# A two-block transformer kernel: comparisons ahead of the weight split, and the mixer's and the layer boundaries' weight work in another order

## The chip, the cores and the metric

One core of one Trainium2 chip runs the whole kernel in one launch. The time is the device time of the launch in microseconds (us), taken as the median over runs; lower is better.

## The reference, cut to what matters

256 tokens of width 1024 in fp32 go through two blocks.

```python
def reference(x, ...):
    h = x
    for i in range(2):                        # first block
        m = diff_attention(h) if i == 0 else short_gated_conv(h)
        h = layer_norm(ALPHA * h + m)
        h = layer_norm(ALPHA * h + swiglu(h))
    x = h                                     # second block
    x = x + parallel_mixer(rms_norm(x))       # 4 mLSTM heads, 8 stick-breaking heads, then w_out
    x = x + memory_cross_attention(rms_norm(x), rms_norm(mem))
    x = x + peer_ffn(rms_norm(x))
    return rms_norm(x)

def peer_ffn(xt):                             # 16384 experts, 8 heads, 16 experts per head and token
    experts, gates = top16(product_keys(xt @ wq))
    act = gelu(einsum('cd,ced->ce', xt, u[experts])) * gates
    return einsum('ce,ced->cd', act, v[experts])
```

`parallel_mixer` puts its mLSTM queries and keys through a causal depthwise convolution of four taps with a bias, then silu; both kinds of head are normalised per head before `w_out`. `mem` is a second sequence of 256 tokens, normalised and projected to keys and values of the cross-attention.

## The kernel before, in words

**Weights.** All weight matrices come as one stream (class `Stream`, L198 to L260) of 1 MB chunks, in a fixed plan. The SyncE queue (SP) loads a chunk into one of two `raw` buffers; each half of it, 128 x 1024, is cast by ScalarE (ACT) into a high part `wh` (L231), and the rest `wl` = raw - wh is formed by VectorE (DVE) or GpSimd (POOL), whichever `W.sub[k]` names for half k (L243). A product is three matmuls, high x high, high x low, low x high (L329, L330, L331). `W.split(n)` brings the split up to half n, `W.pre(n)` the cast alone; asking for half n splits `W.look` halves further on (0, 1 or 2). `wh` and `wl` have three buffers each, and a chunk's buffer is loaded again once both its halves are split.

**Order.** Every engine runs its instructions in the order in which the program writes them; there is no other scheduler. So a line that is written earlier stands ahead on its engine, and an instruction that waits holds up all behind it.

**First block.** The loop over `st` (L776) takes one attention head per step: `qk_proj` projects, `qk_rot` shuffles columns on DVE (L647) and multiplies with the rope tables on POOL (L649, L651, L653), `scores` and `soft` follow one step later. Beside it run `mem_norm` (norm of one half of `mem`), `lam` (the scalar lambda) and `to_T(mem_in)`, which transposes `mem` on TensorE (PE) and splits it into `mT` (high `mTh`, low `mTl`, L378). At the end of each layer, `finish` ends the last matmuls of token half 0, then of half 1, while the norm of half 0 runs, with projections of the memory (`mem_k0`, `mem_k1`, `mem_v`) in between to keep PE at work; `finish_any` (L505) and `finish_two` (L475) set which weights are split there, on which engine.

**Between the blocks.** After the second feed-forward layer, two DMAs on the POOL queue (L965) copy `mT` (2 x 1 MB) to the buffers of an old activation, so that the memory of `mT` can be used for the mixer's tiles.

**Mixer.** `mqk` (L1045) projects one mLSTM head's query and key, and does the convolution on DVE: the first tap and the bias as `tensor_scalar` (L1059), the three others as `scalar_tensor_tensor` (L1062). Meanwhile the halves k = 0 of the weights are split on POOL. `ml_norm` scales the mLSTM heads (L1131), `sb_norm` norms the stick-breaking heads with a product on POOL (L1192) and one on DVE (L1198), `mem_v(2)` projects the memory beside it, and `w_out` ends in a layer boundary again.

**PEER.** All 16384 expert rows of `u` are multiplied with the tokens, in 64 chunks of two halves. The gates of most tokens are scattered by POOL into a zeroed table in DRAM; the gates of the last 128 tokens are made in the last halves of the `u` loop instead, four tokens at a time, in three steps per half: `hot_make` compares an iota with the experts' row and column numbers on DVE (`oi`, L1571; `oj`, L1574), `hot_mm` multiplies the two one-hot tiles on PE (L1581) and writes the result into the table `big`: its finished columns are multiplied on DVE (L1584), the others copied by ACT (L1585). `gelu` (L1592, L1595, L1596) puts the activations into `big`, with a product on DVE or POOL (`late`, run by `gated()`). These halves are called the hot stage below. The loop's order in one half is: split of the weights to come (in `w(k)`), gelu of the last chunk, the product, then `hot_make` for the next half and `hot_mm` of the half before:

```python
            w(k)
...
            proj_stat(ps[:, k * 256:k * 256 + 256], w, k, xT)
...
                if e < 33:
                    hot_make(e - 1)
                gated()
                if e > 1:
                    hot_mm(e - 2, 2 * c)
```

The `v` rows follow as 64 more chunks, with the table `big` as the other factor.

## Time and profile before

| what | value |
|---|---|
| median of 3 runs | 1720.41 us (1719.59 to 1721.41) |
| the profiled execution | 1723.32 us, of it the span 1721.5 us |
| granted TensorE clock, mean over the span | 0.992 of full |
| PE busy with matmuls | 1656.5 us, 96% of the span |
| DVE busy | 1175.8 us, 68% |
| ACT busy | 815.0 us, 47% |
| POOL busy | 483.2 us, 28% |
| DMA | 317.48 MB, 184 GB/s over the span |

The profile is of one execution, 0.17% longer than the median. The shares are averages over stages with different limits: where PE idles is read from stretches of the trace, and what it waits for from the releaser that the trace puts down at each idle time. A matmul row gives the start and the modelled length; matmuls overlap, so the distance between starts tells what one costs.

### The profile page before, as it was taken

How to read it: one execution, taken by the hardware profiler on the slowest of the kernel's cores; microseconds unless marked ns; L12 is line 12 of the kernel's file. 1: busy time of each engine (PE TensorE's matmuls, PEld its weight loads, DVE VectorE, ACT ScalarE, POOL GpSimd, SP SyncE). 2: the span in 40 equal slices, each digit the busy share in tenths (PEclk: the TensorE clock that was granted, in tenths of full speed). 3: DMA queues.
4: the chain of work that ended last, by engine and by line, in shares of the span. 5: the costliest groups of instructions: out<-in, count | busy, mean ns of one | idle time of the engine just before them, and what ended most of it. 6: DMA issues, size and time to landing. Idle time of an engine off the chain costs nothing.

```text
span 1721.5 us, 27583 instructions
## 1 busy us (share of the span) xinstructions
PE 1656.5 (96%) x11013; PEld 1505.5 (87%) x11013; DVE 1175.8 (68%) x2069; ACT 815.0 (47%) x1260; POOL 483.2 (28%) x446
## 2 busy tenths in 40 slices
PE   8899999999999998998999999999888999999997
PEld 7888999899999977887989999999887888888886
DVE  5897554667654564776558889888777666666665
ACT  5564444434444444564445545445332444444544
POOL 0542000200200022203037887788501211111111
PEclk9999999999999999999999999999999999999999
DMA  7346776455555545434355676766433566666664
GB/s 272 137 140 231 256 237 234 172 208 200 207 182 196 177 166 192 164 104 145 122 193 167 178 196 176 193 181 188 100 121 101 188 219 206 209 219 209 207 217 171
DMA packets 80416, 317.48 MB, mean 184 GB/s; under 512 B 25120, under 2 KB 41760, under 8 KB 45344
## 3 DMA queue, kind: packets, MB, share of 16 engines
q1 hardware_dynamic: 59120, 304.38, 51.7%
q0 software_dynamic: 20736, 10.56, 4.1%
q8 instruction: 86, 1.41, 0.3%
q10 hardware_dynamic: 432, 0.79, 0.1%
q14 instruction: 42, 0.34, 0.1%
HBM read 303.04 MB, written 10.55 MB: 182 GB/s over the span
## 4 chain that ended last, share of the span: by engine, by line
PE 47%; DVE 8%; issue 3%; ACT 3%; POOL 1%; DMA 1%; POOLq 0%; DVEq 0%; ACTq 0%
PE acc L331 8%; PE acc L330 7%; PE acc L329 7%; PE mm L329 7%; PE mm L331 7%; PE mm L330 7%; ACT wh L231 2%; DVE oj L1574 2%; DVE oi L1571 1%; DVE big L1584 1%; DVE wl L243 1%; DMA xTl<-mTl 1%; DVE qkm L1062 1%; POOL wl L243 0%; PE mm L1460 0%
## 5 line engine op out<-in xcount | busy, mean ns | idle before, releaser
L243 DVE TENSOR_TENSOR wl<-raw,wh 128x1024 fp32r<-128x1024 f32 (+1 forms) x511 | 631.5, 1254 | 301.6 <-ACT wh L231 300.3
L231 ACT ACTIVATE wh<-raw 128x1024 fp32r<-128x1024 f32 (+1 forms) x537 | 552.6, 1053 | 377.4 <-PE acc L331 181.7
L329 PE MATMUL mm<-xTh,wh 128*128 128x256 f32 x2328 | 660.2, 284 | 1.1 <-DVE mTl L378 1.1
L331 PE MATMUL mm<-xTh,wl 128*128 128x256 f32 x2328 | 655.8, 282 | 1.8 <-DVE wl L243 1.5
L330 PE MATMUL mm<-xTl,wh 128*128 128x256 f32 x2328 | 655.3, 281 | 0.0
L329 PEld LDWEIGHTS mm<-xTh,wh 128*128 128x128 f32 x2328 | 441.6, 190 | 3.9 <-DVE mTl L378 1.5
L331 PEld LDWEIGHTS mm<-xTh,wl 128*128 128x128 f32 x2328 | 441.3, 190 | 2.7 <-DVE wl L243 1.9
L330 PEld LDWEIGHTS mm<-xTl,wh 128*128 128x128 f32 x2328 | 441.5, 190 | 0.9
L1492 POOL DMA_INDIRECT gd<-slots,idx x128 | 259.9, 2030 | 68.9 <-issue 32.3
L329 PE MATMUL acc<-wh,xTh 128*128 128x512 f32 x632 | 249.7, 395 | 0.0
L330 PE MATMUL acc<-wl,xTh 128*128 128x512 f32 x632 | 249.2, 394 | 0.2 <-DVE wl L243 0.2
L243 POOL TENSOR_TENSOR wl<-raw,wh 128x1024 fp32r<-128x1024 f32 x26 | 64.6, 2491 | 566.8 <-ACT wh L231 565.2
L331 PE MATMUL acc<-wh,xTh 128*128 128x512 f32 x504 | 201.1, 399 | 0.0
L330 PEld LDWEIGHTS acc<-wl,xTh 128*128 128x128 f32 x632 | 119.1, 188 | 30.2 <-DVE wl L243 0.8
L329 PEld LDWEIGHTS acc<-wh,xTh 128*128 128x128 f32 x632 | 119.0, 188 | 28.7 <-issue 0.7
L1539 POOL TENSOR_TENSOR big<-big,oj 128x256 f32<-128x256 f32 x64 | 57.5, 898 | 290.3 <-DMA oj<-gd 290.3
L331 PEld LDWEIGHTS acc<-wh,xTh 128*128 128x128 f32 x504 | 94.6, 188 | 21.7
L880 DVE TENSOR_TENSOR sil<-sil,mm 128x256 f32<-128x256 f32 x44 | 18.5, 421 | 102.7 <-ACT sil L879 102.7
L879 ACT ACTIVATE sil<-mm 128x256 f32<-128x256 f32 x44 | 16.9, 385 | 148.4 <-PE mm L331 148.4
L362 DVE TENSOR_TENSOR xTh<-big,xTh 128x256 fp32r<-128x256 f32 x126 | 79.4, 630 | 0.0
L1491 POOL MEMSET spacer<- 1x1 f32 x128 | 78.9, 616 | 0.0
L330 PE MATMUL acc<-wl,hTh 128*128 128x512 f32 x176 | 69.6, 395 | 0.0
(388 smaller groups left out, 1844.2 us busy)
## 6 DMA issues: line engine op xcount, KB each, us to landing
raw<-in_ws_dram SPq DMA_DIRECT2D x131, 1024.0 KB, 5.1
raw<-in_us_dram SPq DMA_DIRECT2D x64, 1024.0 KB, 5.1
raw<-in_vs_dram SPq DMA_DIRECT2D x64, 1024.0 KB, 4.9
gd<-zt SPq DMA_DIRECT2D x32, 256.0 KB, 6.9
raw<-in_pq_dram SPq DMA_DIRECT2D x8, 1024.0 KB, 4.9
oj<-gd SPq DMA_DIRECT2D x64, 128.0 KB, 4.8
gb<-in_vec_dram POOLq DMA_DIRECT2D x12, 512.0 KB, 7.1
gd<-slots,idx POOLq DMA_INDIRECT x128, 4.0
```

The costliest lines, as they stand in the source:

```text
L231: self.nc.scalar.activation(h[:, s], self.R[i][:, k * HW:(k + 1) * HW][:, s], AF.Copy)
L243: self.sub[k].tensor_tensor(l[:, s], self.R[i][:, k * HW:(k + 1) * HW][:, s], h.bitcast(F32)[:, s], op=OP.subtract)
L329: P.matmul(ps, lh, rh, start=first, stop=False)
L330: P.matmul(ps, lh, rl, start=False, stop=False)
L331: P.matmul(ps, ll, rh, start=False, stop=last)
L362: V.tensor_tensor(l, src, h.bitcast(F32), op=OP.subtract)
L880: V.tensor_tensor(s, s, pg[:, 256:], op=OP.mult)
L1062: V.scalar_tensor_tensor(y[:, a, :], pad[:, a, j:j + 256], cols[:, 24 + 4 * ft + j:25 + 4 * ft + j], y[:, a, :], op0=OP.mult, op1=OP.add)
L1491: G.memset(spacer, 0.0)
L1492: d = G.indirect_dma_start(out=gd, out_offset=bass.IndirectOffsetOnAxis(ap=idx[:, h, k:k + 1], axis=0), in_=gate[:, 0, h, k:k + 1], in_off ...
L1539: G.tensor_tensor(b, b, GT.pop(c), op=OP.mult)
L1574: V.tensor_scalar(oj[:, i, :], iota, ET[:, 1, t:t + 1], ET[:, 2, t:t + 1], op0=OP.is_equal, op1=OP.mult)
```

## The change

Nothing is computed otherwise; work is put elsewhere in the order, on another engine, or in other pieces.

1. A half that POOL splits is subtracted in four pieces of 256 columns instead of one instruction of 1024 (`Stream.split`).
2. `finish_two` no longer splits the first half of the next chunk on POOL ahead of the norm of token half 0; it is split later with the second half.
3. `finish_any`, in its `early` form, only casts there, and subtracts after the norm's first part of both token halves.
4. In the first attention heads the column shuffle of head 0 stands ahead of the weight split, of the memory's second norm and of lambda; the transposes of `mem` go ahead of a weight split and the softmax's second part.
5. The copy of `mT` is issued ahead of the last layer boundary of the first block instead of behind it.
6. In `mqk` the first tap is done by ACT, and all weight halves are split on DVE.
7. `ml_norm` is split in two: token half 1 ahead of `sb_z`, half 0 behind it; `sb_c(5)` goes ahead of a transpose.
8. `sb_norm` multiplies in four pieces on POOL; the weights next to it are split on DVE, with `W.look` at 1 for `mem_v(2)`.
9. In the hot stage `hot_make` stands ahead of `w(k)`, and so ahead of the weight split.

```diff
@@ -239,7 +239,10 @@
             h, l = self.T[self.ns]
-            for s in self.parts(self.ns):
+            ps = self.parts(self.ns)
+            if self.sub[k] is self.nc.gpsimd:
+                ps = [slice(q, q + 256) for q in range(0, HW, 256)]
+            for s in ps:
                 self.sub[k].tensor_tensor(l[:, s], self.R[i][:, k * HW:(k + 1) * HW][:, s], h.bitcast(F32)[:, s],
@@ -475,8 +478,6 @@
         last_mm(acc, items, 1, 1)
-        W.sub = [G, G]
-        W.split(2 * W.i + 3)
         W.sub = [G, G]
@@ -519,11 +520,14 @@
             last_mm(acc, items, 1, 1)
-            W.split(2 * W.i + first + early)
+            W.pre(2 * W.i + first + early)
         fa(1, 0)
...
         fa(1, 1)
+        if early:
+            W.sub = [V, G]
+            W.split(W.np - 1)
         if callable(src0):
@@ -772,13 +776,10 @@
     mem_norm(0)
-    mem_norm(1)
     for st in range(8 + 5):
...
             qk_proj(st)
-        if st == 0:
-            lam()
         if st == 8:
@@ -800,6 +801,8 @@
             W.split(2 * W.i + 4)
+            mem_norm(1)
+            lam()
         if 0 <= st - 1 < 8:
@@ -807,13 +810,13 @@
                 pv_n(st - 4)
+            if st in (1, 2):
+                to_T(mem_in[st - 1], st - 1, mT)
             W.split(2 * W.i + 4)
...
             soft(st - 1)
-        if st in (1, 2):
-            to_T(mem_in[st - 1], st - 1, mT)
 
@@ -958,11 +961,12 @@
 
+    mT2 = new_xT()
+    for k in range(2):
+        G.dma_start(mT2[k], mT[k])
     finish(acc, items, lambda t, nb: ln_a(t, nb, acc, h3), ln_rms, xT, [lambda: mem_v(0)], [lambda: mem_v(1)], True, early=0)
     f2ctx.close()
-    mTo, mT = mT, new_xT()
-    for k in range(2):
-        G.dma_start(mT[k], mTo[k])
+    mT = mT2
     mctx.close()
@@ -1056,8 +1060,8 @@
             ft = a * 4 + h
-            V.tensor_scalar(y[:, a, :], pad[:, a, 0:256], cols[:, 24 + 4 * ft:25 + 4 * ft], cols[:, 56 + ft:57 + ft],
-                            op0=OP.mult, op1=OP.add)
+            A.activation(y[:, a, :], pad[:, a, 0:256], AF.Identity, bias=cols[:, 56 + ft:57 + ft],
+                         scale=cols[:, 24 + 4 * ft:25 + 4 * ft])
             for j in range(1, 4):
@@ -1123,12 +1127,10 @@
 
-    def ml_norm(ss):
-        rs = inv_sqrt(ss, 8, "rs8")
-        for t in (1, 0):
-            for h in range(4):
-                hs = slice(h * 128, h * 128 + 128)
-                V.tensor_scalar(mixed[:, t, hs], mixed[:, t, hs], rs[:, 4 * t + h:4 * t + h + 1], None, op0=OP.mult)
+    def ml_norm(rs, t):
+        for h in range(4):
+            hs = slice(h * 128, h * 128 + 128)
+            V.tensor_scalar(mixed[:, t, hs], mixed[:, t, hs], rs[:, 4 * t + h:4 * t + h + 1], None, op0=OP.mult)
 
@@ -1189,7 +1191,8 @@
             A.activation(sq, mixed[:, t, 512:], AF.Square)
-            G.tensor_tensor(mixed[:, t, 512:], mixed[:, t, 512:], gmx[:, 512:], op=OP.mult)
+            for c in (slice(512, 768), slice(768, 1024)):
+                G.tensor_tensor(mixed[:, t, c], mixed[:, t, c], gmx[:, c], op=OP.mult)
             V.tensor_reduce(ss[:, 8 * t:8 * t + 8], sq.rearrange("p (a b) -> p a b", a=8), axis=AX.X, op=OP.add)
@@ -1207,7 +1210,6 @@
         A.activation(vx[:, t, :, 0:128], pss[t].rearrange("p (a b) -> p a b", a=4), AF.Copy)
-    W.sub = [G, V]
     for h in range(4):
@@ -1230,7 +1232,8 @@
         if hs == 6:
-            ml_norm(ss8)
+            rs8 = inv_sqrt(ss8, 8, "rs8")
+            ml_norm(rs8, 1)
         i, k = divmod(hs - 2, 2)
@@ -1238,6 +1241,8 @@
                 sb_z(i)
+                if hs == 6:
+                    ml_norm(rs8, 0)
             elif i < 2:
@@ -1252,8 +1257,8 @@
     sb_c(4)
+    sb_c(5)
     to_T_half(mixed[:, 0, :], 0, mxT, 0)
-    sb_c(5)
     acc = acc_banks()
@@ -1266,12 +1271,12 @@
     sb_v(7)
-    W.sub = [G, V]
     sb_norm()
+    W.look = 1
     mem_v(2)
-    W.sub = [V, V]
     for t in range(2):
         to_T_half(mixed[:, t, :], t, mxT, 1)
+    W.look = 2
     items = o_items(mxT, "wout", 2)
@@ -1607,6 +1612,9 @@
         for k in range(2):
+            e = 2 * c + k - HOT0
+            if 1 <= e < 33:
+                hot_make(e - 1)
             w(k)
@@ -1618,18 +1626,13 @@
             pump(CRED1)
-            e = 2 * c + k - HOT0
             if e >= 0:
...
                 hot_T()
-            if 1 <= e < 34:
-                if e < 33:
-                    hot_make(e - 1)
-                gated()
-                if e > 1:
-                    hot_mm(e - 2, 2 * c)
             gated()
+            if 2 <= e < 34:
+                hot_mm(e - 2, 2 * c)
         pend.append(lambda c=c, ps=ps: gelu(c, ps))
```

On DVE in the hot stage the kernel before has, from the end of one step to the start of the next, the last comparisons of a step (`oj`), the late product of the gelu (`gx`), the product into `big`, the weight split and the next comparison (`oi`):

```order
L1574 TENSOR_SCALAR oj<-cst,ET 128x128 x4
L1596 TENSOR_TENSOR big<-big,gx 128x2x44
L1584 TENSOR_TENSOR big<-big,acc_13539 128x104x4
L243 TENSOR_TENSOR wl<-raw,wh 128x1024
L1571 TENSOR_TENSOR oi<-cst,ET 128x512
```

In the changed kernel, at the same place on DVE:

```order
L1601 TENSOR_TENSOR big<-big,gx 128x2x44
L1589 TENSOR_TENSOR big<-big,acc_13595 128x104x4
L1576 TENSOR_TENSOR oi<-cst,ET 128x512
L1579 TENSOR_SCALAR oj<-cst,ET 128x128 x4
L246 TENSOR_TENSOR wl<-raw,wh 128x1024
```

The comparisons now stand between the product into `big` and the next split, where the split followed the product at once.

On POOL at the end of the first block, the kernel before has the loads of norm vectors (`gb`), a weight split, the norms of the two token halves (`rs`, `h`), and the copy behind them:

```order
L301 DMA gb<-in_vec_dram 128x1024 x3
L243 TENSOR_TENSOR wl<-raw,wh 128x1024
L320 TENSOR_TENSOR rs_6562<-rs1a,nhalf 128x1
L426 TENSOR_TENSOR h<-r,gb 128x512 x2
L320 TENSOR_TENSOR rs_6606<-rs1a,nhalf 128x1
L243 TENSOR_TENSOR wl<-raw,wh 128x1024
L320 TENSOR_TENSOR rs_6624<-ssa,nhalf 128x1
L320 TENSOR_TENSOR rs_6635<-ssa,nhalf 128x1
L243 TENSOR_TENSOR wl<-raw,wh 128x1024 x2
L965 DMA xTh_6705<-mTh 128x2048
L965 DMA xTl_6706<-mTl 128x2048
```

In the changed kernel POOL has:

```order
L304 DMA gb<-in_vec_dram 128x1024 x3
L966 DMA xTh_6514<-mTh 128x2048
L966 DMA xTl_6515<-mTl 128x2048
L323 TENSOR_TENSOR rs_6586<-rs1a,nhalf 128x1
L429 TENSOR_TENSOR h<-r,gb 128x512 x2
L323 TENSOR_TENSOR rs_6630<-rs1a,nhalf 128x1
L246 TENSOR_TENSOR wl<-raw,wh 128x256 x8
L323 TENSOR_TENSOR rs_6658<-ssa,nhalf 128x1
L323 TENSOR_TENSOR rs_6669<-ssa,nhalf 128x1
L246 TENSOR_TENSOR wl<-raw,wh 128x256 x8
```

The copy moved ahead of the norms and of four weight halves, and the split that stood ahead of the first `rs` moved behind the second, where two halves now follow as eight pieces.

On DVE in `mqk` the kernel before has, from the second part of one head (`qkm` is a head's query and key; each has two parts) to the first part of the next, one weight half, the other being on POOL:

```order
L1059 TENSOR_SCALAR qkm_7014<-r_7011,cols_86 128x256
L1062 SCALAR_TENSOR_TENSOR qkm_7014<-r_7011,cols_86,qkm_7014 128x256 x3
L243 TENSOR_TENSOR wl_7054<-raw_6924,wh_7052 128x1024
L1059 TENSOR_SCALAR qkm_7085<-r_7082,cols_86 128x256
L1062 SCALAR_TENSOR_TENSOR qkm_7085<-r_7082,cols_86,qkm_7085 128x256 x3
```

In the changed kernel DVE has, for two heads:

```order
L246 TENSOR_TENSOR wl_6983<-raw_6895,wh_6981 128x1024
L246 TENSOR_TENSOR wl_7019<-raw_6895,wh_7017 128x1024
L1066 SCALAR_TENSOR_TENSOR qkm_7050<-r_7047,cols_86,qkm_7050 128x256 x6
L246 TENSOR_TENSOR wl_7062<-raw_6960,wh_7060 128x1024
L246 TENSOR_TENSOR wl_7090<-raw_6960,wh_7088 128x1024
L1066 SCALAR_TENSOR_TENSOR qkm_7121<-r_7118,cols_86,qkm_7121 128x256 x6
```

The first taps are gone from DVE, and the second weight half of each head is there instead.

## Rows read from the trace of the kernel before

**Rows 1.** Stretches: us busy (x instructions) of PE, PEld, DVE, ACT, POOL; PEclk; DMA share; GB/s.

```profile
1280.00:1300.00 20.00, 16.06 (x129) 15.30 (x128) 15.04 (x31) 5.79 (x12) 2.09 (x3) 1.00 0.32 106
665.88:671.60 5.72, 5.72 (x14) 4.46 (x15) 2.36 (x2) 4.21 (x5) 0.00 (x0) 0.50 0.21 47
60.00:80.00 20.00, 18.86 (x159) 17.84 (x158) 19.45 (x43) 12.37 (x35) 12.03 (x9) 1.00 0.44 158
```

**Rows 2.** Timeline of PE, hot products: start us, us, engine, line, operation [idle before <-releaser].

```profile
1199.99 1.05 PE L1581 MATMUL acc<-oj,oi 128*128 128x128 f32 x8
...
1211.11 1.05 PE L1581 MATMUL acc<-oj,oi 128*128 128x128 f32 x8
...
1343.53 1.17 PE L1581 MATMUL acc<-oj,oi 128*128 128x128 f32 x8 [0.62 <-DVE oj L1574]
```

**Rows 3.** Timeline of DVE in the hot stage.

```profile
1265.51 0.68 DVE L1571 TENSOR_TENSOR oi<-cst,ET 128x512 f32<-128x512 f32 x1
1266.12 1.11 DVE L1574 TENSOR_SCALAR oj<-cst,ET 128x128 f32<-128x128 f32 x4
1267.14 0.59 DVE L1584 TENSOR_TENSOR big<-big,acc 128x424 f32<-128x424 f32 x1
1268.99 1.23 DVE L243 TENSOR_TENSOR wl<-raw,wh 128x1024 fp32r<-128x1024 f32 x1 [1.26 <-ACT wh L231]
1270.13 0.93 DVE L1571 TENSOR_TENSOR oi<-cst,ET 128x512 f32<-128x512 f32 x1
```

**Rows 4.** Timeline of ACT in the hot stage.

```profile
1267.77 0.24 ACT L1585 ACTIVATE big<-acc 128x88 f32<-128x88 f32 x1 [3.43 <-DVE big L1584]
```

**Rows 5.** Timeline of POOL in the hot stage.

```profile
1269.58 0.94 POOL L1596 TENSOR_TENSOR big<-big,gx 128x120 f32<-128x120 f32 x1 [8.55 <-ACT gx L1595]
```

**Rows 6.** Chain of waits, 640 to 700 us: start us, us, what.

```profile
650.19 14.93 DMA xTl<-mTl
```

**Rows 7.** Waits of PE, 600 to 900 us: us in total, times, longest us.

```profile
PE mm L329 <- ACT vs L1002: 4.4, 1, 4.4
PE mm L370 <- ACT xTh L373: 3.0, 1, 3.0
PE mm L1204 <- DVE h L1198: 2.2, 1, 2.2
PE mm L370 <- DVE r L448: 1.9, 1, 1.9
PE mm L330 <- DVE wl L243: 1.6, 2, 0.8
...
PE acc L1169 <- DVE spv L1163: 1.2, 1, 1.2
```

**Rows 8.** DMA issues, 640 to 670 us: KB each, us to landing.

```profile
raw<-in_ws_dram SPq DMA_DIRECT2D x4, 1024.0 KB, 7.8
```

**Rows 9.** DMA issues of the whole span, from the page.

```profile
raw<-in_ws_dram SPq DMA_DIRECT2D x131, 1024.0 KB, 5.1
```

**Rows 10.** Timeline of DVE at the first block's end.

```profile
623.40 2.36 DVE L243 TENSOR_TENSOR wl<-raw,wh 128x1024 fp32r<-128x1024 f32 x2 [3.12 <-ACT wh L231]
...
628.75 3.36 DVE L422 SCALAR_TENSOR_TENSOR r<-r,mv,gb 128x512 f32<-128x512 f32 x2
...
635.10 1.41 DVE L422 SCALAR_TENSOR_TENSOR r<-r,mv,gb 128x512 f32<-128x512 f32 x2
```

**Rows 11.** Timeline of POOL at the first block's end.

```profile
628.50 2.39 POOL L243 TENSOR_TENSOR wl<-raw,wh 128x1024 fp32r<-128x1024 f32 x1 [182.03 <-ACT wh L231]
```

**Rows 12.** Timeline of DVE in mqk.

```profile
693.53 0.41 DVE L1059 TENSOR_SCALAR qkm<-r,cols 128x256 f32<-128x256 f32 x1
...
695.42 2.54 DVE L1059 TENSOR_SCALAR qkm<-r,cols 128x256 f32<-128x256 f32 x1
```

**Rows 13.** Timeline of POOL in mqk.

```profile
695.07 2.69 POOL L243 TENSOR_TENSOR wl<-raw,wh 128x1024 fp32r<-128x1024 f32 x1 [5.24 <-ACT wh L231]
```

**Rows 14.** Waits of PE, 0 to 130 us.

```profile
PE acc L664 <- POOL qk L653: 3.7, 2, 3.4
```

## The prediction

> **What bounds the kernel now.** The sum is made against the profiled execution, 1723.3 us, of which 1721.5 us are the span; it is 0.17% above the median of 1720.4 us, so savings are taken from both alike. The page comes first: PE is busy in 96% of the span, so a change pays only where PE stands still or runs at half its clock. The stretches come next, 20 us each. Through most of the kernel PE is busy in nearly all of each. In the hot stage it is not: 16.06 us of 20 (the first of [rows 1]), while DVE has 15.04 and ACT 5.79, so no engine is full and a chain of waits goes in a circle. The third view is the waits of PE, which gives the other places [rows 7, 14].
>
> The circle is read from the timelines. The products of the hot stage that stand unhindered start 3.71 us apart: three steps from 1199.99 to 1211.11 [rows 2]. From then on PE comes to wait for `oj` in each step, and 32 steps in all end at 1343.53, where 31 steps of 3.71 from 1199.99 would have ended at 1314.9. So **28.6 us** are lost there. On DVE, `oi` takes 0.61 us from start to start, the four `oj` 1.02, the product into `big` 0.59 [rows 3]. Only when `big` ends, at 1267.73, can ACT copy the other columns, at 1267.77 [rows 4], and behind that copy it casts the next weights. DVE's weight split waits for the cast, 1.26 us idle, and takes 1.14 to the next `oi` [rows 3]. The circle is 1.14 + 0.61 + 1.02 + 0.59 + 1.26 = 4.62; from 1211.11 to 1343.53, 28 steps, it is 4.73 [rows 2]. The last 0.11 is put down to POOL: an `oi` that runs beside POOL's product of the gelu [rows 5] takes 0.93 where another takes 0.68 [rows 3], in every second step.
>
> **Part 9, the comparisons first.** Nothing is added. `oi` and `oj`, 1.63 us, move into the time in which ACT copies and casts, where DVE was idle for 1.26. Then DVE no longer waits: its step is 1.14 + 0.61 + 1.02 + 0.59 = 3.36, with POOL's 0.11 it is 3.47, under PE's 3.71. ACT's share, the 5.79 us in a stretch of 20 (first of [rows 1]), stays. The comparisons' own inputs are made once, ahead of the stage. PE becomes the bound, as it was in the first steps, and all of 28.6 goes but for the settling: **-28**. If POOL's product of 0.94 us (one in two steps) were to hold DVE up for its full length on top of that, DVE's step would be 3.47 + 0.47 = 3.94 and PE would lose 31 x 0.23 = 7: the lower bound is -21.
>
> **Part 5, the copy of mT.** The chain of waits has 14.93 us of this copy on it [rows 6]: PE stands still for 4.4 us behind it [rows 7], and then runs at a granted clock of 0.50, the lower of its two levels, for 5.72 us (second of [rows 1]), in which half, 2.86, is lost. Issued before the last layer boundary, when POOL is idle, the copy is done long before the mixer wants the memory: 4.4 + 2.86 = 7.3 saved. It costs where it goes. Loads of weights beside it took 7.8 us to land [rows 8], against 5.1 for this stream over the span [rows 9]. The last weights of the second feed-forward layer and the first of `mem_v` then land up to 2.7 us late, and on DVE the split of the latter (first of [rows 10]) stands ahead of the norm's first instruction, which delays the norm by as much.
>
> **Part 2** gives some of it back at the same place. While the POOL split ran [rows 11], a pair of norm instructions on DVE took 3.36 us; the same pair of token half 1, with no split beside it, took 1.41 [rows 10]. So the norm of half 0 is 1.95 earlier, at the same place. The two halves of `mem_v(1)` are then split late, in eight pieces behind the second norm, and may keep PE waiting for 0 to 3 us. I take -1.3 off the saving for all three: **-6** for the place, between -2 and -7.3. At the three boundaries before it, the same order stays and PE hardly waits there: 0.
>
> By the Trainium skill, "DMA: Bandwidth & Descriptors", section on queues, rings and completion order, each DMA engine takes turns between the queues that have work, a packet at a time. That speaks against an earlier copy: beside two megabytes of it, weight loads would be halved in speed, and by that rule alone this term would be rival A's, 0 in the place of -6. The trace agrees in direction, 7.8 against 5.1 [rows 8, 9], not by a factor of two; no run here shows the new place.
>
> **Parts 1 and 6, mqk.** With a POOL split of 2.69 us running [rows 13], a first tap on DVE that takes 0.41 takes 2.54 [rows 12]. In the changed kernel DVE has two splits and six taps for a head: 2 x 1.14 + 6 x 0.41 = 4.7, an estimate that gives every tap the first one's price. PE needs for a head's two products at least 2 x (3.71 - 1.05) = 5.3, the step of the hot stage less its hot products [rows 2]. So PE bounds, and its waits for the split, 1.6 [rows 7], go: **-1.6** (0, if the other taps are dearer, to -2). The first taps on ACT lie beside this, since ACT is idle for over half of most stretches [rows 1].
>
> **Part 7.** PE waits 1.2 for the stick-breaking weights behind eight multiplications of `ml_norm` [rows 7]; half of them move behind. **-0.6** (0 to -1.2).
>
> **Parts 1, 3 and 8, the boundaries of the second block.** PE waits 2.2 at the stick-breaking norm and 3.0 at the next norm's transposes [rows 7], both behind DVE instructions that share their time with POOL splits, as in `mqk`. Part 8 moves one split off POOL, part 3 puts the two of the boundary behind the norm's sums, and the rest comes in four pieces, so that a DVE instruction meets a quarter of one. That should halve the waits; `W.look` at 1 makes the first weights of `w_out`'s rest late, which takes a part again. **-2.6** (0 to -5.2). Behind the cross-attention, where part 3 holds too, PE waits 1.9 [rows 7], and a quarter of that is taken as POOL's: **-0.5** (0 to -1.9).
>
> **Part 4, the first heads.** PE waits 3.7 for the first heads' rope on POOL [rows 14], which follows a shuffle that is now earlier. But in the heads behind, DVE is busy for 19.45 of 20 us and bounds them (third of [rows 1]), and the moved work, the second norm and lambda, still has to be done on it before they end. Most of the gain is waited away: **-0.5** (+1.5 to -3.7).
>
> **Sum:** 28 + 6 + 1.6 + 0.6 + 2.6 + 0.5 + 0.5 = 39.8, so 1720.4 - 39.8 = **1680.6 us**, and the profiled execution would be 1683.5.
>
> **The rivals.** *A: the copy costs as much as it saves.* Where the weights behind the copy were the last to arrive and the clock fell once more, the 6 us would be gone, with the part of part 2: 1686.6. For it: the loads of 7.8 us [rows 8] and the split ahead of the norm [rows 10]. Against it: most of the weights of the stage are loaded before. *B: the hot stage ends on DVE, not on PE.* If POOL's product blocks DVE for its full length, -21 in the place of -28: 1687.6. For it: POOL is shown to stretch an `oi` [rows 3, 5]. Against it: the stretch measured is 0.25 of 0.94. By the Trainium skill, "SBUF — State Buffer", section "Who interferes with whom", GpSimd and some DVE instructions, those with two operands in SBUF among them, share a port pair that one holds for a whole instruction while the other blocks. That rule with POOL first is B, -21. In `mqk` the trace agrees (2.54 in the place of 0.41 beside 2.69 [rows 12, 13]); in the hot stage, 0.25 of 0.94, only in part.
>
> *C, the slower side: weights become late in the hot stage.* Now 1.63 us of comparisons stand ahead of every split. If the product of a step waited for the split issued just before it, the step would be 3.71 + 1.63 = 5.34, and 31 of them 165.5 us against the 143.5 between the first and last product now [rows 2]: +22, less the 11.8 of the other parts, 1730.6. It decides if the splits run less than one step ahead; `W.look` is 2 there, so they run two, 7.4 us of PE's time, and PE waits for `oj` alone in this stage. That the order does not do what is written can be left out, since the pieces of order show it.
>
> **How the numbers follow.** Forecast 0.63; A alone 0.16; B alone 0.14; A and B 0.04 (1693.6); C 0.02; and 0.01 that the small parts and the copy take back what the hot stage gives. All the others but C are faster. What a measurement of this kernel can tell from no change is about 0.2%, 3.4 us. Faster 0.97, same 0.01, slower 0.02. The forecast's own bounds are -50 (28.6, 7.3, 2, 1.2, 5.2, 1.9, 3.7 together) and, with B, -21.5 (21 and 2, the rest 0, +1.5), but not all ends come at once: the range is **1672 to 1692**, which holds the forecast, A and B.
>
> **What the profile will show.** Right: in the hot stage the products start 3.71 us apart to the end, PE has 20 of 20 us, DVE waits for nothing but PE's result, and the last product comes some 28 us earlier against the first. The chain no longer holds the copy, `vs` follows its matmuls at once, and the clock stays up in the mixer. In `mqk` no tap on DVE takes over 0.6. Wrong: PE still idle ahead of `oj`; or idle for the split, which would be C; a PE wait at the new place of the copy, ahead of `mem_v`; `mem_v(1)` waiting for POOL.

## The result and the profile after

The changed kernel takes 1692.84 us (median of 4 runs, 1692.53 to 1694.92), the kernel before on the same chip 1720.0 (4 runs, 1717.75 to 1721.41): a ratio of 0.9846, interval 0.9829 to 0.9863. It is faster by 27 us, where 39.8 were forecast, and the time lies 0.8 us above the stated range. The profiled executions differ by more, 1692.53 against 1723.32; the sums below are of these two, so some 3.6 us of their 30.8 are a difference between executions.

The hot stage did what its working said. The first fence has its products on PE, as in [rows 2]: start, length, engine, line.

```profile
1199.48 1.05 PE L1586 MATMUL acc<-oj,oi 128*128 128x128 f32 x8
...
1310.72 1.05 PE L1586 MATMUL acc<-oj,oi 128*128 128x128 f32 x8
1314.43 1.05 PE L1586 MATMUL acc<-oj,oi 128*128 128x128 f32 x8
```

From first to last it is 114.95 us, 31 steps of 3.71, against 143.54 before: 28.6 saved. DVE's timeline, as in [rows 3], shows why:

```profile
1241.89 0.68 DVE L1576 TENSOR_TENSOR oi<-cst,ET 128x512 f32<-128x512 f32 x1
1242.49 1.11 DVE L1579 TENSOR_SCALAR oj<-cst,ET 128x128 f32<-128x128 f32 x4
1243.52 1.22 DVE L246 TENSOR_TENSOR wl<-raw,wh 128x1024 fp32r<-128x1024 f32 x1
1245.09 0.59 DVE L1589 TENSOR_TENSOR big<-big,acc 128x416 f32<-128x416 f32 x1 [0.36 <-PE acc L1586]
```

The split no longer waits for the cast; the one idle time left is for PE's result, 0.36 us. In the stretch (columns as in [rows 1]) PE is now busy for all of 20 us:

```profile
1280.00:1300.00 20.00, 20.00 (x175) 20.00 (x174) 18.53 (x40) 7.79 (x17) 3.36 (x3) 1.00 0.43 140
```

So the missing 12 us were lost elsewhere. To find the places, the start of one and the same PE instruction in the two profiles is compared; the lag is the time after less the time before, negative where the changed kernel is ahead. A step of this table is what a stretch gained or lost.

| place (us in the kernel before) | lag of the changed kernel | step | forecast |
|---|---|---|---|
| 117, end of the attention heads | -0.6 | -0.6 | -0.5 |
| 345, second layer boundary | -0.9 | -0.3 | 0 |
| 353, first chunks behind it | +1.9 | **+2.8** | 0 |
| 443, third layer boundary | +1.85 | 0 | 0 |
| 460, first chunks behind it | +6.35 | **+4.5** | 0 |
| 597, second feed-forward | +6.2 | -0.2 | 0 |
| 646, end of the first block | +10.9 | **+4.7** | +1.3 |
| 673, behind the copy | +3.3 | -7.5 | -7.3 |
| 720, behind `mqk` | +0.1 | -3.3 | -1.6 |
| 765, stick-breaking | +0.5 | +0.5 | -0.6 |
| 812 to 879, two boundaries | -5.2 | -5.7 | -3.1 |
| 897, start of PEER | -0.4 | **+4.8** | 0 |
| 1344, end of the hot stage | -29.1 | -28.7 | -28 |

The four bold steps give back 16.8 us. Behind the hot stage some 1.8 more are won, 0.82 of it a wait of PE at the first `v` product that is gone. Three causes were read from the two traces.

**Behind the second and third boundary PE waits for weights.** The rows at the third are, in the kernel before, of POOL and of ACT:

```profile
440.17 4.74 POOL L243 TENSOR_TENSOR wl<-raw,wh 128x1024 fp32r<-128x1024 f32 x2 [2.43 <-ACT wh L231]
...
450.53 2.01 ACT L231 ACTIVATE wh<-raw 128x1024 fp32r<-128x1024 f32 x2 [0.77 <-DMA raw<-in_ws_dram]
```

And in the changed kernel, of POOL, SP, ACT and PE:

```profile
442.02 7.58 POOL L246 TENSOR_TENSOR wl<-raw,wh 128x256 fp32r<-128x256 f32 x8 [2.44 <-ACT wh L231]
...
449.63 0.80 SPq L215 DMA_DIRECT2D raw<-in_ws_dram  x2
...
456.59 2.00 ACT L231 ACTIVATE wh<-raw 128x1024 fp32r<-128x1024 f32 x2 [4.86 <-DMA raw<-in_ws_dram]
...
457.70 0.38 PE L332 MATMUL mm<-xTh,wh 128*128 128x256 f32 x1 [1.60 <-ACT wh L231]
...
458.96 0.53 PE L334 MATMUL mm<-xTh,wl 128*128 128x256 f32 x1 [0.76 <-DVE wl L246]
```

The two halves take 7.58 us as eight pieces and 4.74 as two whole instructions. A raw buffer is loaded again only when both halves are split, so the next chunk is asked for later, its cast starts 6.1 us later at a lag of 1.85, and PE waits 1.60 and 0.76; from 458 to 464 us its clock is 0.72 of full on average, before it was 1.00. Of the 4.2 us beyond the lag, 2.8 are the pieces. That the other 1.4 come from the load itself is argued: SP now issues this chunk and the next 0.4 us apart, where they were 2.2 apart (444.94 and 447.16) before.

**At the end of the first block** PE waits for POOL, in the list of PE's waits (us in total, times, longest), the counterpart of [rows 7]; the `vs` wait of 4.4 is gone:

```profile
PE mm L333 <- POOL wl L246: 3.5, 1, 3.5
PE mm L373 <- DVE r L451: 3.1, 2, 1.8
PE mm L334 <- POOL wl L246: 2.6, 1, 2.6
```

The first is `mem_v(1)`, whose two halves POOL splits only behind the second norm; the stretch behind it runs at the lower clock. In the rows of DVE, POOL, PE and the stretch, the first is the counterpart of the first of [rows 10], the split ahead of the norm:

```profile
632.90 2.36 DVE L246 TENSOR_TENSOR wl<-raw,wh 128x1024 fp32r<-128x1024 f32 x2 [5.14 <-ACT wh L231]
...
643.77 6.57 POOL L246 TENSOR_TENSOR wl<-raw,wh 128x256 fp32r<-128x256 f32 x8
...
645.81 0.80 PE L333 MATMUL mm<-wl,mTh 128*128 128x512 f32 x1 [3.53 <-POOL wl L246]
...
644.00:648.00 4.00, 2.19 (x5) 1.82 (x6) 2.80 (x5) 1.55 (x6) 4.00 (x5) 0.50 0.00 0
```

**At the start of PEER** a store stands in the way (timelines of POOL, SP, ACT, DVE and PE, and one stretch):

```profile
874.16 0.61 POOL L1368 DMA_DIRECT2D hs<-h  x1
...
874.24 0.33 SPq L215 DMA_DIRECT2D raw<-in_pq_dram  x1
...
883.37 0.60 ACT L1457 ACTIVATE big<-mm 128x512 f32<-128x512 f32 x1 [5.46 <-DMA hs<-h]
...
884.02 0.54 POOL L1382 DMA_DIRECT2D big<-in_subk_dram  x1 [9.26 <-ACT big L1457]
884.57 5.55 POOL L246 TENSOR_TENSOR wl<-raw,wh 128x256 fp32r<-128x256 f32 x8
...
884.94 6.26 DVE L246 TENSOR_TENSOR wl<-raw,wh 128x1024 fp32r<-128x1024 f32 x1 [8.60 <-ACT wh L231]
...
885.37 0.38 PE L334 MATMUL mm<-xTh,wl 128*128 128x256 f32 x1 [2.62 <-POOL wl L246]
...
886.00:890.00 4.00, 4.00 (x24) 4.00 (x24) 4.00 (x1) 0.21 (x1) 4.00 (x7) 0.61 0.89 336
```

`hs` is the residual, stored to DRAM from memory that the table `big` takes over. ACT's first write into `big` waits for the store's end, POOL's queue waits at the subkeys' load for ACT, and PE waits for the split behind that load. In the kernel before PE reached this place 5.2 us later, and ACT's write waited for PE.

What makes the store's end late is the weight load beside it. The split just ahead of the store frees a raw buffer, so SP issues the next load 0.08 us behind the store, and the load goes first. From 874 to 879 us and from 879 to 883 us the two queues moved (q1 is SP's, q0 POOL's; packets, MB, share of 16 engines):

```profile
q1 hardware_dynamic: 105, 0.86, 71.2%
q0 software_dynamic: 4, 0.03, 1.5%
...
q0 software_dynamic: 140, 1.02, 60.1%
q1 hardware_dynamic: 39, 0.19, 12.8%
```

### The profile page after: what moved, and what is told of

Same layout as the page of the kernel before. It is cut to its first block, busy times and chain, and to the rows that moved or that the text cites. A ratio compares the mean times of both kernels' runs of the same rounds, so it can differ in the third digit from the quotient of the medians.

```text
span 1690.6 us, 27640 instructions
## 1 busy us (share of the span) xinstructions
PE 1645.0 (97%) x11013; PEld 1500.1 (89%) x11013; DVE 1164.4 (69%) x2069; ACT 818.4 (48%) x1268; POOL 471.1 (28%) x494
## 3 DMA queue, kind: packets, MB, share of 16 engines
q8 instruction: 86, 1.41, 0.3%
## 4 chain that ended last, share of the span: by engine, by line
PE 83%; DVE 6%; issue 3%; POOL 3%; ACT 2%; DMA 2%; POOLq 0%; ACTq 0%; DVEq 0%
PE mm L334 16%; PE mm L332 16%; PE mm L333 16%; PE acc L333 10%; PE acc L332 10%; PE acc L334 9%; DVE wl L246 3%; PE acc L1586 2%; DMA raw<-in_ws_dram 1%; POOL wl L246 1%; ACT wh L231 1%; POOL rs L323 1%; DMA hs<-h 1%; POOL h L429 0%; PE mm L1341 0%
## 5 line engine op out<-in xcount | busy, mean ns | idle before, releaser
L246 DVE TENSOR_TENSOR wl<-raw,wh 128x1024 fp32r<-128x1024 f32 (+1 forms) x519 | 642.2, 1256 | 271.7 <-ACT wh L231 269.7
L1497 POOL DMA_INDIRECT gd<-slots,idx x128 | 253.2, 1978 | 62.6 <-issue 32.2
L246 POOL TENSOR_TENSOR wl<-raw,wh 128x256 fp32r<-128x256 f32 x72 | 56.9, 825 | 325.0 <-ACT wh L231 325.0
L332 PE MATMUL acc<-wh,hTh 128*128 128x512 f32 x176 | 69.6, 395 | 0.0
```

The costliest lines, as they stand in the source:

```text
L246: self.sub[k].tensor_tensor(l[:, s], self.R[i][:, k * HW:(k + 1) * HW][:, s], h.bitcast(F32)[:, s], op=OP.subtract)
L332: P.matmul(ps, lh, rh, start=first, stop=False)
L1497: d = G.indirect_dma_start(out=gd, out_offset=bass.IndirectOffsetOnAxis(ap=idx[:, h, k:k + 1], axis=0), in_=gate[:, 0, h, k:k + 1], in_off ...
```

## The experiments

Three theories were put to the test against each other: that the **pieces** (part 1) are slow on POOL and make the next load late; that the **late split** (part 2) costs what is lost at the first block's end; and the prediction's rival A, that the **copy** (part 5) costs at its new place what it saves. The lags below are against the one profile of the kernel before. Two executions of the same code differ, too: e4, which has the old code up to 1200 us, leads by 1 to 2 us there, so steps are compared and not single lags. A step can differ as well: e4, with the old code, loses 1.2 from 879 to 897.

| lag at | changed | e1 | e2 | e3 | e4 | e5 | e6 | e8 | e9 | e10 | e12 |
|---|---|---|---|---|---|---|---|---|---|---|---|
| 345 | -0.9 | -1.2 | -0.9 | -1.2 | -1.1 | 0.0 | -0.6 | -1.4 | -0.9 | -0.4 | -1.1 |
| 460 | +6.4 | -1.5 | +6.3 | -1.8 | -1.6 | +7.7 | -1.0 | -1.7 | -1.5 | -0.4 | -1.4 |
| 597 | +6.2 | -1.5 | +6.5 | -1.9 | -1.7 | +7.9 | -1.1 | -1.6 | -1.5 | -0.4 | -1.3 |
| 646 | +10.9 | +3.3 | +7.3 | -1.8 | -1.7 | +8.7 | -1.1 | +0.1 | +0.2 | -0.2 | -1.0 |
| 673 | +3.3 | -4.2 | 0.0 | -9.2 | -2.1 | +8.3 | -0.9 | -7.4 | -7.4 | -7.6 | -8.4 |
| 720 | +0.1 | -7.5 | -3.3 | -12.4 | -2.1 | +6.1 | -4.2 | -10.6 | -10.6 | -10.9 | -11.7 |
| 765 | +0.5 | -7.1 | -2.9 | -12.0 | -2.1 | +6.3 | -3.8 | -10.2 | -10.2 | -10.4 | -11.2 |
| 879 | -5.2 | -8.0 | -8.4 | -13.0 | -2.2 | +4.5 | -3.7 | -10.0 | -15.9 | -11.3 | -16.6 |
| 897 | -0.4 | -4.8 | -3.8 | -8.2 | -1.0 | +7.7 | -0.5 | -9.4 | -9.3 | -10.8 | -12.7 |
| 1344 | -29.1 | -33.4 | -32.5 | -36.8 | -29.6 | +7.8 | -29.3 | -37.9 | -37.8 | -39.4 | -41.3 |

**e1, whole splits.** Part 1 undone:

```diff
-            ps = self.parts(self.ns)
-            if self.sub[k] is self.nc.gpsimd:
-                ps = [slice(q, q + 256) for q in range(0, HW, 256)]
-            for s in ps:
+            for s in self.parts(self.ns):
```

> The changed kernel with POOL's weight splits whole again (part 1 undone). Theory P: the four pieces make two halves take 7.58 us on POOL in the place of 4.74, so the raw buffer comes free 2.8 us later, the next chunk lands later, and PE waits for its cast behind the second and third layer boundary; this alone gave away 7.0 us there. Undone, PE's lead of 0.8 us over the kernel before should last to the end of the first block's feed-forward (before: lag of 6.2 us), and the time is about 1685.5 us (1683 to 1687.5). Rival: the loads are late because of the order (moved transposes, moved splits), and the time stays at 1692.8 within 1.

1689.69 us against 1721.87 before, ratio 0.9822 (0.9805 to 0.9838). The time is above what was expected, but the two places are as theory P has it: the lead of 1.2 us at 345 lasts to 597, at -1.5. POOL's row and the cast at the third boundary are

```profile
438.58 4.75 POOL L243 TENSOR_TENSOR wl<-raw,wh 128x1024 fp32r<-128x1024 f32 x2 [2.44 <-ACT wh L231]
...
450.34 2.01 ACT L231 ACTIVATE wh<-raw 128x1024 fp32r<-128x1024 f32 x2 [2.21 <-DMA raw<-in_ws_dram]
```

and PE has no wait. The rest of the expectation failed because the pieces do help later: from 765 to 879 us e1 wins 0.8 where the changed kernel wins 5.7. At the first block's end e1 loses 4.8, as the changed kernel does, so that loss doesn't need the pieces; PE waits 4.0 for the whole split there.

**e2, the early split back.** Part 2 undone, in pieces:

```diff
+        W.sub = [G, G]
+        W.split(2 * W.i + 3)
         W.sub = [G, G]
         r0 = fb(0)
```

> The changed kernel with the split of one weight half ahead of the norm of token half 0 again (part 2 undone), in four pieces. Theory S: PE's wait of 3.53 us for POOL's split in the second memory projection, and the half clock behind it, come from the late split alone: 3 to 5 us are won, 1688 to 1690 us. Rival P: the split is late there because the pieces are slow and the norm itself is late behind the copy, so that an earlier place wins 0 to 2 us, 1691 to 1692.8.

1688.16 us, ratio 0.9812 (0.9792 to 0.9832), as theory S has it. From 597 to 646 us it loses 0.9 where the changed kernel loses 4.7, and no other step moved by more than 0.3. PE's waits for POOL there are 1.43 and 0.18:

```profile
645.95 0.50 PE L333 MATMUL mm<-wl,mTh 128*128 128x512 f32 x1 [1.43 <-POOL wl L246]
...
647.79 0.50 PE L333 MATMUL mm<-wl,mTh 128*128 128x512 f32 x1 [0.18 <-POOL wl L246]
```

**e3, both.**

> The changed kernel with both undone: whole splits, and the early split ahead of the norm. If P and S are both right and add up, 1681 to 1683 us. If one covers for the other, it stays at the better of the two, about 1685. What is left against the kernel before at the end of the first block is then the copy's own cost: the norm starts after weights that land beside the copy, 3 us late in the changed kernel.

1686.17 us, ratio 0.9802 (0.9786 to 0.9819). Neither the boundaries nor the first block's end lose anything now (-1.9 at 597, -1.8 at 646), and all of the copy's 7.4 is won behind it. The time is 3 to 5 us above the sum of the two theories, since whole splits give up the gain at 765 to 879 us.

**e4, part 9 alone.**

```diff
         for k in range(2):
+            e = 2 * c + k - HOT0
+            if 1 <= e < 33:
+                hot_make(e - 1)
             w(k)
...
-            if 1 <= e < 34:
-                if e < 33:
-                    hot_make(e - 1)
-                gated()
-                if e > 1:
-                    hot_mm(e - 2, 2 * c)
             gated()
+            if 2 <= e < 34:
+                hot_mm(e - 2, 2 * c)
```

> The kernel before with part 9 alone. Theory: the hot stage is independent of the rest, its products start 3.71 us apart, and it saves 28.6 us in the stage and 1 to 2 behind it: 1690 us (1689 to 1692). Then all other parts of the change together are worth about nothing in the changed kernel (within 3 us). Rival: the stage gains only with the rest, for instance because the scatter on POOL ends earlier there: above 1695.

1691.5 us, ratio 0.9825 (0.9808 to 0.9841): as fast as the whole change, within the intervals. The hot products run from 1198.95 to 1313.89, 114.94 us again. So the eight other parts together were worth nothing that these runs can tell.

**e5, part 1 alone** on the kernel before, the same edit as in e1 the other way round.

> The kernel before with part 1 alone: POOL's splits in four pieces. Theory P: two halves on POOL take 2.8 us longer at the second and third boundary, the raw buffer comes free later, and PE lags 6 to 8 us behind the kernel before from 460 us on, all of it at these two places. Behind that, in the mixer, where DVE waited for POOL's whole splits, 0 to 5 us come back. 1722 to 1728 us against 1720 to 1722 for the kernel before. Rival: the lag of the changed kernel there needs its earlier order too, and the pieces alone change nothing before 600 us.

1730.81 us against 1721.92, ratio 1.0056 (1.0039 to 1.0073): slower than expected, and slower beyond doubt. PE lags 7.7 us at 460, all of it at the two boundaries, with none of the other parts there:

```profile
443.85 7.59 POOL L246 TENSOR_TENSOR wl<-raw,wh 128x256 fp32r<-128x256 f32 x8 [2.11 <-ACT wh L231]
...
459.19 0.39 PE L332 MATMUL mm<-xTh,wh 128*128 128x256 f32 x1 [1.33 <-ACT wh L231]
```

Of the 0 to 5 us that were to come back, 2.1 came in `mqk` and 1.8 from 765 to 879, and 3.2 were lost again at the start of PEER.

**e6, the copy at its old place,** on e3:

```diff
-    mT2 = new_xT()
-    for k in range(2):
-        G.dma_start(mT2[k], mT[k])
     finish(...)
     f2ctx.close()
-    mT = mT2
+    mTo, mT = mT, new_xT()
+    for k in range(2):
+        G.dma_start(mT[k], mTo[k])
```

> e3_whole_early with the copy of mT at its old place behind the last boundary (part 5 undone). In e3_whole_early PE's lead stayed at 1.8 us over the boundary and grew by 7.35 behind the copy. If the early copy costs nothing there, this kernel is 7.3 us slower than e3_whole_early, about 1693.5 where that had 1686.2. Rival A of the prediction, the copy costs at its new place what it saves: within 1.5 us of e3_whole_early, and the boundary itself shorter.

1691.79 us, ratio 0.9821 (0.9805 to 0.9838), 5.6 above e3's median. The intervals of the two ratios overlap, but the four times of each do not (1685.34 to 1688.12 and 1689.6 to 1692.95); rival A, within 1.5, falls. PE waits 4.42 us again, and between 646 and 673 us nothing is won, where e3 won 7.4:

```profile
664.86 0.80 PE L329 MATMUL mm<-wh,xTh 128*128 128x512 f32 x1 [4.42 <-ACT vs L1004]
```

The copy is not quite free at its new place: over the boundary (597 to 646) e6 loses 0.0, e3 0.1, and e8 and e9, with the same code there as e3, 1.7 each. That fits a cost of 0 to about 2 us, differing by execution: PE's wait for POOL's split there is 0.8 in e3 and 1.8 in e8 and e9.

**e8, the store of hs early,** on e3, in two halves, each behind the norm of its token half:

```diff
+    def rms_hs(t):
+        r = rms_b(h6[:, t, :], ("ss", t), gf)
+        G.dma_start(hs[:, t, :], h6[:, t, :])
+        return r
...
-    G.dma_start(hs, h6)
```

> e3_whole_early with the store of the residual hs in two DMAs, each issued right behind the norm of its token half, in the place of one DMA behind both. Theory H: at the start of PEER POOL's queue stands behind the subkeys' load, which waits with ACT for the store's end (5.46 us in the changed kernel), so POOL's split comes late, PE waits and falls to half its clock; 4.8 us of lead are lost between the cross-attention's end and the second query product. With the store some 3 to 6 us earlier, 3 to 4.8 us are won: about 1682. Rival: the loss comes from the weight loads beside the store and stays: 1686 within 1.

1684.78 us, ratio 0.9787 (0.977 to 0.9803). The time lies between the two expectations. Theory H holds for the place: from 879 to 897 us 0.7 are lost, not 4.8. The rival is right about what made the store late. Ahead of the split, with no load beside it, each half lands in 2.9 us:

```profile
hs<-h POOLq DMA_DIRECT2D x2, 512.0 KB, 2.9
```

The whole store behind the split took until ACT's write, 9.2 us, in the changed kernel. But 2.0 us went one step earlier, between 861 and 879 us, where e3 lost 1.0; the expectation had not seen that, and e10 shows how.

**e9, pieces only in the second block's two boundaries,** on e3. A flag `fine` of the stream switches them on ahead of `mem_v(2)` and off behind the cross-attention's boundary:

```diff
-            if self.sub[k] is self.nc.gpsimd:
+            if self.fine and self.sub[k] is self.nc.gpsimd:
```

> e3_whole_early with four pieces only at the two boundaries of the second block (behind the mixer and behind the cross-attention), whole splits elsewhere. The lead grew by 5.7 us between 779 and 879 us with pieces in the changed kernel, by 1.0 with whole splits. If the pieces help there because DVE's norm waits for one piece and not for a whole split, 3.5 to 5 us are won: about 1682. Rival: that gain came from being late before (the changed kernel had more weights loaded ahead): within 1 of e3_whole_early.

1684.7 us, ratio 0.9784 (0.9768 to 0.98), less than expected. From 765 to 879 us it wins 5.7, so the pieces do help there by themselves; but the store of `hs` then takes 6.6 back, where e3 lost 4.8. ACT waits 5.30 us for it:

```profile
872.53 0.60 ACT L1462 ACTIVATE big<-mm 128x512 f32<-128x512 f32 x1 [5.30 <-DMA hs<-h]
```

**e10, e9 and e8 together.**

> Both of the last two together: pieces only at the two boundaries of the second block, and the store of hs early. In e9 PE's lead was 15.9 us behind the cross-attention's end, and 6.6 of it were lost while the store ended; in e8 only 0.7 were lost there. If the store's end is the barrier that ate the pieces' gain, the lead at 897 us is 13 to 15 us in the place of 9.3, and the time 1679 to 1681 us with the kernel before at 1721.9. Rival: another load at the start of PEER holds PE (the subkeys), and the lead falls to 9 to 10 again: 1684.5.

1681.13 us (5 runs) against 1721.28, ratio 0.9765 (0.9751 to 0.9778). The store's end no longer shows at the start of PEER (0.5 lost), but the lead at 897 is 10.8 and not 13 to 15, mainly because the boundary ahead of it lost 2.5 where e9 had gained 0.6. The rows of DVE and POOL there are

```profile
862.13 3.57 DVE L452 TENSOR_SCALAR r<-r,rs 128x512 f32<-128x512 f32 x1 [0.69 <-POOL rs L324]
...
862.06 0.57 POOL L1372 DMA_DIRECT2D hs<-h  x1
862.65 2.76 POOL L247 TENSOR_TENSOR wl<-raw,wh 128x256 fp32r<-128x256 f32 x4
```

The DVE instruction that starts 0.07 us behind POOL's issue of the second store ends at 865.70, 0.3 us behind the last of the four pieces.

**e11, the copy in the middle,** on e10, issued behind the norm of token half 1.

> e10 with the copy of mT issued behind the norm of token half 1 instead of ahead of the boundary: later than the last weights of the feed-forward and of the memory projection, earlier than at first. In e3, e8 and e9 the weights of the memory projection landed 2 us late beside the copy, and PE's lead fell by 0 to 1.7 us over the boundary. If that is the copy's cost, 0 to 1.7 us are won. Rival: the copy then ends too late for the mixer's memory (it took 14.9 us beside loads, and is wanted some 18 us behind that norm), and 0 to 3 us are lost.

1681.94 us, ratio 0.9769 (0.9755 to 0.9782): no difference from e10 that the intervals can tell. By steps it loses 1.0 from 597 to 646 us (-1.4 to -0.4), where e10 lost 0.2, and wins 7.3 behind the copy, as e10 did. So the expected gain did not come. The 1.0 goes another way: a pair of DVE instructions beside the split that follows the copy's issue takes 4.53 us, in e10 3.52, and PE waits 1.7 for POOL's next split, in e10 0.9.

**e12, the second store back behind the pieces.**

```diff
-        G.dma_start(hs[:, t, :], h6[:, t, :])
+        if t == 0:
+            G.dma_start(hs[:, 0, :], h6[:, 0, :])
...
+    G.dma_start(hs[:, 1, :], h6[:, 1, :])
```

> e10 with only the first half of hs stored early; the second half's store goes behind POOL's last weight split of that boundary again. In e10 a DVE instruction of the last norm took 3.57 us in the place of 0.94: it began while POOL issued the second store and came free only with all four pieces behind it, and PE waited 3.9 in the place of 1.3. If that store ahead of the pieces is the cause, the instruction takes under 1 us again, PE's lead behind the boundary is 15 us in the place of 11.3; of this, 1 to 3 us are lost to the second store's end, half as long as before: 1679 to 1680.5 with the kernel before at 1721.3. Rival: the second half's store ends as late as the whole one did, and the lead falls to 9 or 10: 1683 to 1684.5.

1681.12 us (5 runs) against 1721.21, ratio 0.977 (0.9756 to 0.9783). The DVE instruction takes 0.95 again, with the same pieces beside it:

```profile
859.89 0.95 DVE L452 TENSOR_SCALAR r<-r,rs 128x512 f32<-128x512 f32 x1 [0.69 <-POOL rs L324]
...
859.84 2.98 POOL L247 TENSOR_TENSOR wl<-raw,wh 128x256 fp32r<-128x256 f32 x4
```

The lead is 16.6 us behind the boundary, and 3.9, not 1 to 3, are lost to the second half's store, which now goes beside the next load: ACT waits for its end until 7.3 us behind its issue. So the time misses the expected 1679 to 1680.5, and in the times e10 and e12 are the same. Both are about 0.8% under the changed kernel by their ratios, 0.9765 and 0.977 against 0.9846, and beat both kernels.

## Why the prediction was wrong

**The hot stage, right.** The term was -28, measured -28.6 in the stage. Rival B, that POOL's product holds DVE up for its length, did not come about: products stay 3.71 us apart in all 31 steps. Rival C, late weights, did not either: PE has no wait in the stage. The estimate of DVE's step, 3.47, is close: DVE now waits 0.32 us a step for PE (0.2 to 0.4), so its own step is 3.39.

**The boundaries of the first block, wrong, and the largest miss.** The step that failed is "At the three boundaries before it, the same order stays and PE hardly waits there: 0". The order stayed, but the pieces made the splits longer, and the prediction put that at nothing without a reason: part 1 had a term only where it helps. Two halves take 7.58 us and not 4.74, which [rows 10, 11] could not show, and the load behind them is tied to the buffer they free. It cost 7.3 us (2.8 + 4.5). e5 has the same loss from part 1 alone, and e1 and e3 have none: shown.

**Part 2, wrong in size.** The step is "may keep PE waiting for 0 to 3 us. I take -1.3 off the saving for all three". The wait was 3.53 us, outside that bound, with the lower clock behind it; the place lost 4.7. It is the prediction's own sign of being wrong, "`mem_v(1)` waiting for POOL". With part 2 undone the place lost 0.9 in pieces and 0.1 whole (e2, e3): shown. With the copy's gain the place is at -2.8, inside the bounds of -2 to -7.3 that were given for it. The gain that was set against it, a norm 1.95 us earlier, was there (the pair of norm instructions takes 1.41), and did not matter, since PE waited for the split.

**Part 5, the copy, right.** 7.3 were forecast, 7.5 came. That weights beside it land late was right as well: the split ahead of the norm started 3.3 us later than the lag ahead of it explains, 9.5 against 6.2 (632.90 against 623.40). In the changed kernel that lateness reaches PE by part 2: POOL's split stands directly behind the late norm on its queue, so the 3.3 us must be in the wait of 3.53 too. No run has part 2 without the early copy, so how the 4.7 divide between parts 2 and 5 stays open. With part 2 undone the copy costs PE 0 to about 2 us, and rival A, which had a chance of 0.16, is refuted by e6. By the Trainium skill, "DMA: Bandwidth & Descriptors", section on queues, rings and completion order, the engines take turns between queues; it gave rival A, and the runs agree with the slower loads (7.7 us beside the copy in e1), not with the loss. At the start of PEER the trace shows no such turns, 0.86 MB against 0.03; whether the store's packets were ready by then is not shown.

**The start of PEER, missing.** No term and no rival was there for it. The prediction followed a lead of PE from place to place as if nothing fixed were ahead, though the store of `hs` and the subkeys' load stand on POOL's queue there. The loss was 4.8 us; e8 without the whole store behind the boundary lost 0.7: shown. The store ends late because the next weight load goes first (0.86 MB against 0.03 from 874 to 879 us); in the kernel before it had ended when PE came. PE's lateness alone does not hide it: in e5 PE comes 4.5 us behind the kernel before, ACT still idles 2.49 us for the store's end, and 3.2 are lost, though 1.2 of such a step can be the execution's (e4).

**The mixer, right in direction.** `mqk` gave 3.3 for 1.6 and the two boundaries behind it 5.7 for 3.1. `ml_norm` and the transposes behind it lost 0.5 for a gain of 0.6; PE's wait fell from 1.2 to 0.5, and 0.7 came anew at a transpose's low part (not tried further). For the first heads the -0.6 at 117 us looks like the -0.5 of the forecast, but it is not shown to be a gain: e4 and e5, with the old order there, are at -1.0 and +0.2. A lead of 3.6 us at 48 us was waited away by 117, as was forecast.

**The sum.** Forecast -39.8; the four losses that were given 1.3 in it took 16.8, which is 15.5 more, and the terms that were too small gave back some 6. By the profiles it is -30.8. The prediction's number for A and B together, 1693.6, lies 0.8 us from the measured time; neither came about, so that is luck.

## What to carry to other kernels

Before an instruction is cut in pieces, find who waits for its **end**: four pieces can let the other engine in sooner, but a buffer that is freed by the last one comes free later, and here a load hung on that. A time that PE wins early lasts only to the next thing that is tied to something other than PE, so follow the lead down the queues (a store's end, a load behind it, the split behind that) before it is added up. When a change has many parts, the lag of one and the same instruction between two profiles finds the parts that lose.

## What the runs showed that was not expected

Cutting a POOL subtract of 128 x 1024 in four made it longer by unequal amounts: 2.98 and 2.76 us for four pieces at the cross-attention's end (e12, e10), where a whole one took 2.34 (e3), and 7.58 for eight at the third boundary while DVE ran two splits, where two whole ones took 4.74. By the Trainium skill, "SBUF — State Buffer", section "Who interferes with whom", GpSimd and certain DVE instructions hold their shared ports for a whole instruction; so a waiting DVE instruction should get in behind one piece. In e12 it does, 0.95 us beside pieces of about 0.75; in e10, where POOL issued a DMA just ahead of the pieces, it took 3.57 and came free only behind all four. The changed kernel has it again at the start of PEER: directly behind the issue of the subkeys' load DVE's split takes 6.26 us and ends behind all eight pieces, and in e3 it takes 5.41 beside two whole splits there. With no issue just ahead, as at the third boundary, two splits of DVE get in between the pieces and take 3.29 together. Every kept trace agrees with this, so the place of the issue decides; what in it changes the turn stays open.
